# Twelve products of zeros and a written order in the first stage of a two-layer trunk

## The chip, the core and the metric

The kernel runs on one core of one Trainium2 chip. A core has TensorE (PE, matrix products; its weight loads are listed as PEld), VectorE (DVE), ScalarE (ACT), GpSimd (POOL) and SyncE (SP), which here issues nearly all loads. Each engine works through its own list of instructions in order and waits where an operand or a buffer is not ready. The metric is the time of one execution on the device, in microseconds (us).

## The reference

The program takes x (512 tokens of 1024 numbers, f32) through two layers. Each layer is a token mixer and a SwiGLU block; each of these four sub-layers has the same frame:

```python
shift, scale, gate = ada_modulation(c, ada_w, ada_b)   # silu(c) @ w + b, cut in three
h = rms_norm(x, pre_g) * (1.0 + scale) + shift
y = mixer_or_ffn(h)
x = x + gate * rms_norm(y, post_g)
```

The first mixer is an attention: `h @ w_qkv` gives q, k and v (16 heads of 64), a stick-breaking product takes the place of a softmax, and `w_o` projects the result. The second mixer is a gated multiplication over positions. The change touches only what lies ahead of the first attention, and one row of the first gate.

## The kernel before

The tokens lie in four tiles of 128 (`NT`), the features in eight blocks of 128 (`KD`). Products are done in f32 precision by splitting each operand into a high and a low part (`split`: ACT copies the high part, DVE subtracts it from the source for the low part) and adding three products (`mm3`). Weights come in one load each of 512 KB into one of two buffers (`raw`), are split into `wh` and `wl` (`wemit`, DVE at L184), and the next load goes out when a buffer is free. `wget` asks for the next weight.

**The first stage** makes `h`, transposed, and begins q, k and v.

- `norm0(tt)`: ACT squares and sums a tile of x, and takes the root (`sd`); DVE takes the reciprocal (`r`) and scales the tile in place.
- `turn0(tt)`: eight transposes on PE (tile `tp`, L119) into two banks of PSUM, and four copies of 128x256 into `xhT`. For tiles 0 and 1 two copies are ACT's and two DVE's; for tiles 2 and 3 all four are ACT's.
- `row0(raws)`: shift and scale of one block of features, as a row: eight f32 products with one weight column each (tile `ab`; every f32 product shows as two instructions in the trace), a copy of the row by DVE (`row`), and two small products that turn the row into two columns.
- `scales` and `h0`: DVE makes the factors (`ab`) from the columns; ACT writes `hTh` and the scaled `xhT`, DVE subtracts for `hTl`. This is done for block 0 and block 1 from rows; for blocks 2 to 7, `ada0_sum` accumulates on DVE (tile `acc`) and `cols0`/`sums0` reduce on PE.
- `v_step` and `qk0_step` are the products for v (four banks), q and k of the first pair of heads (`pq`, `pk`). All six banks of the tag "b" are then in use.

The order in which an engine takes its instructions is chosen by a planner from estimated durations and readiness, except where the program adds an edge with `order(b, before)`. `Vector`, `Scalar` and `pe_op` have a `chain` flag: while it is set, each new instruction is ordered behind the one before it. In the version before, no chain is set in the first stage; it is set for PE, and later for DVE, from the attention on.

**The gate row.** `Bg` builds a gate, scale or shift row of a later sub-layer in small steps between other work: eight loads of `ada_w` (`rawada`) multiplied into an accumulator on DVE (`ada_stt`), then a load of the row `post_g` or `pre_g` spread over the partitions (tile `g`), and for each half a split (`acch`, `accl`), two products with ones on PE, and DVE's multiplication with `g`. `bg0` builds the first gate, "G0": its eight loads are issued in the first stage, the rest in the attention, where the products go to the banks named `av` and DVE follows a written order.

## Time and profile before

| | us |
|---|---|
| median of 3 runs | 1104.47 (1104.46 to 1104.56) |
| the profiled execution | 1103.49 |
| its span, first to last instruction | 1101.7 |
| PE busy in the span | 1082.1 |
| DVE busy | 972.8 |
| ACT busy | 610.1 |

The three runs lie within 0.1 us of each other; the profiled execution is 1.0 us below their median, and its span 1.8 us below its own time. Rows of the profile begin with start and duration in us when they are in order of time; a bracket at the end tells how long the engine was idle before the row, and what it waited for. `x8` is a count of merged instructions. L89 is the helper by which all of ACT's activations are recorded, L73 that of DVE, L111 that of products, L119 of transposes, L128 of loads.

### The profile page before, as it was taken

To read this page: it belongs to the slowest core of one execution; us is meant where nothing else is said; L and a number is where in the kernel's file an instruction comes from. 1 tells how busy PE (TensorE), PEld (TensorE's weight loads), DVE (VectorE), ACT (ScalarE), POOL (GpSimd) and SP (SyncE) were. 2 spreads that over 40 slices of the span, in tenths; PEclk is the share of its full clock that TensorE was granted. 3 is DMA by queue.
4 is the path that set the end of the run, shared out by engine and by line. 5 is a ranking of instruction groups with operands and counts; after the bars stand their busy time and mean duration, and the time that the engine had idled before them with its cause. 6 is when DMAs were issued, how large, how long until landed. Compare 5 with 4: busy or idle time off the path is not lost.

```text
span 1101.7 us, 18701 instructions
## 1 busy us (share of the span) xinstructions
PE 1082.1 (98%) x7452; PEld 978.7 (89%) x7452; DVE 972.8 (88%) x1293; ACT 610.1 (55%) x1016; POOL 29.5 (3%) x53
## 2 busy tenths in 40 slices
PE   7999999999999999999999999999999999999997
PEld 4787788788999999998888899988999999999996
DVE  4988999866989999989978999868979999899996
ACT  6554665665655555554252767526545555565662
POOL 0020100000000000001000000001000000000000
PEclk9999999999999999999999999999999999999999
DMA  8976434304433434359878324524334342332252
GB/s 317 357 226 218 138 121 131 122 17 153 153 111 124 163 124 153 134 187 347 294 246 322 143 87 137 177 95 163 122 113 153 136 159 100 107 113 96 77 190 78
DMA packets 51355, 176.38 MB, mean 160 GB/s; under 512 B 6074, under 2 KB 9146, under 8 KB 51268
## 3 DMA queue, kind: packets, MB, share of 16 engines
q1 hardware_dynamic: 48708, 166.81, 43.8%
q0 software_dynamic: 2560, 8.39, 2.1%
q8 instruction: 58, 0.95, 0.3%
q14 instruction: 29, 0.24, 0.1%
HBM read 164.69 MB, written 8.39 MB: 157 GB/s over the span
## 4 chain that ended last, share of the span: by engine, by line
PE 85%; DVE 7%; DMA 4%; issue 2%; ACT 2%; SPq 0%; DVEq 0%; ACTq 0%
PE r L111 35%; PE y L111 16%; PE pqk L111 7%; PE X L111 4%; PE gu L111 4%; PE Y L111 3%; PE v L111 3%; PE u L111 2%; PE av L111 2%; PE z L111 2%; PE tw L119 1%; PE Z L111 1%; PE W L111 1%; PE tp L119 1%; DVE wl L184 1%
## 5 line engine op out<-in xcount | busy, mean ns | idle before, releaser
L111 PE MATMUL r<-Sh,wh 128*128 128x256 f32 x640 | 177.3, 277 | 0.6 <-ACT e L89 0.6
L111 PE MATMUL r<-Sl,wh 128*128 128x256 f32 x640 | 177.0, 277 | 0.0
L111 PE MATMUL r<-Sh,wl 128*128 128x256 f32 x640 | 176.9, 277 | 0.0
L89 ACT ACTIVATE wh<-raw 128x1024 fp32r<-128x1024 f32 (+1 forms) x105 | 108.3, 1036 | 101.7 <-DMA raw<-in_wdown 36.1
L111 PE MATMUL y<-wh,as 128*128 128x512 f32 x480 | 150.5, 391 | 0.3 <-DVE svt L73 0.3
L111 PEld LDWEIGHTS r<-Sh,wh 128*128 128x128 f32 x640 | 120.2, 188 | 1.2 <-ACT e L89 1.0
L111 PEld LDWEIGHTS r<-Sl,wh 128*128 128x128 f32 x640 | 120.2, 188 | 0.1
L111 PEld LDWEIGHTS r<-Sh,wl 128*128 128x128 f32 x640 | 120.1, 188 | 0.0
L184 DVE TENSOR_TENSOR wl<-raw,wh 128x1024 fp32r<-128x1024 f32 x79 | 95.9, 1220 | 25.9 <-ACT wh L89 25.7
L73 DVE TENSOR_TENSOR wl<-f,wh 128x1024 fp32r<-128x1024 f32 x95 | 112.9, 1219 | 1.1 <-ACT wh L89 1.1
L89 ACT ACTIVATE wh<-f 128x1024 fp32r<-128x1024 f32 x95 | 100.2, 1055 | 17.3 <-DVE f L73 12.5
L111 PEld LDWEIGHTS y<-wh,as 128*128 128x128 f32 x480 | 90.0, 188 | 19.3 <-issue 0.6
L89 ACT ACTIVATE e<-r 128x256 f32<-128x256 f32 x120 | 45.9, 384 | 102.3 <-PE r L111 100.2
L111 PE MATMUL y<-wl,as 128*128 128x512 f32 x240 | 93.7, 391 | 0.0
L111 PE MATMUL r<-hTh,wh 128*128 128x256 f32 x320 | 88.8, 278 | 0.2 <-DVE gu L73 0.2
L111 PE MATMUL r<-hTh,wl 128*128 128x256 f32 x320 | 88.5, 277 | 0.0
L111 PE MATMUL r<-hTl,wh 128*128 128x256 f32 x320 | 88.5, 277 | 0.0
L111 PEld LDWEIGHTS r<-hTh,wh 128*128 128x128 f32 x320 | 60.1, 188 | 1.1 <-DVE gu L73 0.9
L111 PE MATMUL r<-hTh,b 128*128 128x256 f32 x320 | 60.9, 277 | 0.0
L111 PEld LDWEIGHTS r<-hTl,wh 128*128 128x128 f32 x320 | 60.1, 188 | 0.0
L111 PEld LDWEIGHTS r<-hTh,wl 128*128 128x128 f32 x320 | 60.1, 188 | 0.0
L89 ACT ACTIVATE wh<-rawx 128x1024 fp32r<-128x1024 f32 x40 | 42.5, 1062 | 29.7 <-PE r L111 28.9
(288 smaller groups left out, 2924.3 us busy)
## 6 DMA issues: line engine op xcount, KB each, us to landing
rawada<-in_ada SPq DMA_DIRECT2D x80, 512.0 KB, 6.3
rawy<-in_wy SPq DMA_DIRECT2D x38, 512.0 KB, 4.2
rawx<-in_wx SPq DMA_DIRECT2D x38, 512.0 KB, 3.4
raw<-in_wdown SPq DMA_DIRECT2D x22, 512.0 KB, 5.3
raw<-in_wdn SPq DMA_DIRECT2D x22, 512.0 KB, 3.4
raw<-in_wqk SPq DMA_DIRECT2D x16, 512.0 KB, 4.0
ada<-in_ada0p SPq DMA_DIRECT2D x12, 512.0 KB, 7.6
raw<-in_wgu SPq DMA_DIRECT2D x12, 512.0 KB, 3.5
```

Source lines behind the costliest of these rows:

```text
L73: b = getattr(nc.vector, op)(*args, **kw)
L89: b = nc.scalar.activation(*args, **kw)
L111: b = nc.tensor.matmul(o, l, r, start=start, stop=stop, skip_group_check=True)
L119: last_tp[0] = nc.tensor.transpose(o, i, ident)
L184: last_low[0] = nc.vector.tensor_tensor(l[:], raw[:], h[:].bitcast(F32), ALU.subtract)
```

## The change

Three things are changed.

1. A tile of zeros (128x256) is set by DVE, and `spin(n)` issues n f32 products of it with itself into a bank of their own, which nothing reads. Nine stand ahead of the transposes of tile 0, three between these and the transposes of tile 1.
2. From the first norm on, PE, DVE and ACT follow the order in which the program is written: PE up to the columns of block 0, DVE and ACT up to `h0` of block 0 and the high part of the first q weight. Norms and transposes are cut in two parts so that other work can stand between. The transposes of tiles 2 and 3 stand between the two halves of the first row's products. For all tiles two of the four copies are now DVE's. The low part of the first v weight is ordered behind tile 2's copies and ahead of tile 3's; the low part of the first q weight behind the factors of block 0; the first eight multiply-adds into `acc` behind `hTl` of block 0.
3. For "G0" the load of `g` is issued right behind the last of the eight `rawada` loads, and not when the accumulator is complete.

```diff
+        def row(self, name, s, part):
+
+            if part and name not in self.rows:
+                g = slot(F32, "g", 1, D)[:, 0, :]
+                row = A["pre_g"] if part == 1 else A["post_g"]
+                load(g, row[s : s + 1, :].to_broadcast([P, D]))
+                self.rows[name] = g
+            return self.rows.get(name)
...
                         load(raw, A["ada"][s, part, j % KD])
                         raws.append(raw)
+                        if self.soon and j % KD == KD - 1:
+                            self.row(name, s, part)
...
-                if part:
-                    row = A["pre_g"] if part == 1 else A["post_g"]
-                    g = slot(F32, "g", 1, D)[:, 0, :]
-                    load(g, row[s : s + 1, :].to_broadcast([P, D]))
+                g = self.row(name, s, part)
...
-    bg0, bg = Bg("G0", slots=3, gap=1), Bg("A0", "B0", lag=1, gap=1)
+    bg0, bg = Bg("G0", slots=3, gap=1, soon=True), Bg("A0", "B0", lag=1, gap=1)
...
-                if q and tt < 2:
+                if q:
                     dve.tensor_copy(dst, src)
                 else:
                     act.activation(dst, src, AF.Copy)
...
+    zero = stp.tile([P, 256], F32, name="zero")
+    dve.memset(zero[:], 0.0)
+    zb = bank("zb")
+
+    def spin(n):
+
+        for _ in range(n):
+            mm(zb[:, 0:256], zero[:, 0:P], zero[:], True, True)
...
         for q, raw in enumerate(raws):
+            if q and between is not None:
+                between()
             for k in range(4):
...
-    norm0(0)
-    norm0(1)
-    turn0(0)
-    norm0(2)
-    ab0 = row0(a0)
-    turn0(1)
-    norm0(3)
-    turn0(2)
-    turn0(3)
-    wv0.append(wget(("wv", 0, 0), 0))
+    pe["chain"] = dve.chain = act.chain = True
+    norm0(0)()
+    root = norm0(1)
+    spin(9)
+    turned = turn0(0)
+    root()
+    spin(3)
+    for tt in (2, 3):
+        root = norm0(tt)
+        turned()
+        if tt == 2:
+            turned = turn0(1)
+        root()
+
+    def between():
+        turned = [turn0(tt) for tt in (2, 3)]
+        wv0.append(wget(("wv", 0, 0), 0))
+        for f in turned:
+            f()
+            if f is turned[0]:
+                order(last_low[0], dve.prev)
+                dve.prev = last_low[0]
+
+    ab0 = row0(a0, between)
+    pe["chain"] = False
     a2 = [ada0_raw(2, q) for q in range(4)]
-    h0(scales(ab0, 0), 0, 0)
+    ab = scales(ab0, 0)
+    scaled = dve.prev
+    h0(ab, 0, 0)
+    first = dve.prev
+    wqk0.append(wget(("wqk", 0, 0), 0))
+    order(last_low[0], scaled)
+    dve.chain = act.chain = False
     ab1 = row0(a1)
-    wqk0.append(wget(("wqk", 0, 0), 0))
...
-    acc = ada0_sum(a2, 512, 2)
+    acc = ada0_sum(a2, 512, 2, after=first)
```

`root` and `turned` are the second halves of `norm0` and `turn0`: the root, reciprocal and scaling of a tile, and its copies out of PSUM.

## The prediction

> **What bounds the kernel now.** I read the page first, then what TensorE (PE) waited for, then all engines in order of time up to 31 us, and last the stretch around 90 us.

> ```profile
> span 1101.7 us, 18701 instructions
> PE 1082.1 (98%) x7452; PEld 978.7 (89%) x7452; DVE 972.8 (88%) x1293; ACT 610.1 (55%) x1016; POOL 29.5 (3%) x53
> ...
> PE tp L119 <- DVE x L73: 8.0, 2, 7.3
> PE av L111 <- DVE accl L73: 1.1, 1, 1.1
> ```

> PE is busy for 1082.1 of 1101.7 us. Of its idle time 8.0 us are two waits for the normalised x at the start (7.3 and 0.7), and the next is one of 1.1 us for accl, a half of the gate row. Time is won here only where PE idles or works slowly. The first stage, by PE in order of time, then PE's weight loads around one point:

> ```profile
> 7.31 1.97 PE L119 MATMUL tp<-identt,x 128*128 128x128 f32 x8 [7.31 <-DVE x L73]
> 10.02 1.97 PE L119 MATMUL tp<-identt,x 128*128 128x128 f32 x8 [0.74 <-DVE x L73]
> 11.92 4.96 PE L111 MATMUL ab<-ada,sc 128*1 128x256 f32 x16
> 16.81 0.77 PE L119 MATMUL tp<-identt,x 128*128 128x128 f32 x5
> 17.51 0.60 PE L111 MATMUL ab<-oneb,row 1*128 1x1 f32 x4
> 18.05 1.42 PE L119 MATMUL tp<-identt,x 128*128 128x128 f32 x11
> 19.39 3.61 PE L111 MATMUL ab<-ada,sc 128*1 128x256 f32 x16
> 22.94 0.50 PE L111 MATMUL v<-wh,hTh 128*128 128x512 f32 x1
> ...
> 14.01 0.13 PEld L111 LDWEIGHTS ab<-ada,sc 128*1 128x1 f32 x1 [0.30 <-issue]
> 14.43 0.13 PEld L111 LDWEIGHTS ab<-ada,sc 128*1 128x1 f32 x1 [0.30 <-issue]
> 14.78 0.30 PEld L111 LDWEIGHTS ab<-ada,sc 128*1 128x1 f32 x2 [0.22 <-issue]
> ```

> The same work has two speeds. Each f32 product shows as two passes (eight products, x16). A pass of 256 columns takes 0.42 us up to 14.43 and 0.22 us later (16 from 19.39 to 22.94); a transpose takes 1.90/8 = 0.24 us from 10.02 to 11.92 and 1.34/11 = 0.12 us from 18.05 to 19.39. So PE turns fast at about 14.6 us. The next view, by stretches (columns: us; PE, PEld, DVE, ACT, POOL busy; granted clock; DMA), shows that the granted clock does not tell of it:

> ```profile
> 10.00:14.60 4.60, 4.58 (x15) 2.41 (x16) 3.12 (x8) 4.52 (x11) 0.00 (x0) 1.00 1.03 419
> 19.40:22.90 3.50, 3.50 (x17) 1.25 (x16) 0.69 (x1) 3.44 (x7) 0.00 (x0) 1.00 0.99 405
> 22.00:64.00 42.00, 41.38 (x194) 33.05 (x193) 40.28 (x53) 19.96 (x27) 8.18 (x17) 1.00 0.82 304
> ```

> It reads 1.00 in slow and fast stretches alike; I go by durations. The third row matters most: from 22 to 64 us PE lacks 0.62 us and VectorE (DVE) 1.72 us of 42. An earlier start of v is kept only if DVE starts earlier too. Its rows, with ScalarE's (ACT):

> ```profile
> 13.87 1.06 ACT L89 ACTIVATE wh<-raw 128x1024 fp32r<-128x1024 f32 x1
> 20.23 0.85 ACT L89 ACTIVATE hTh<-xhT,ab 128x512 fp32r<-128x512 f32 x1
> 21.11 0.81 ACT L89 ACTIVATE xhT<-xhT,ab 128x512 f32<-128x512 f32 x1
> ...
> 12.03 0.76 DVE L73 COPY xhT<-tp 128x256 f32<-128x256 f32 x2 [0.30 <-PE tp L119]
> 12.89 0.75 DVE L73 TENSOR_SCALAR x<-x,r 128x1024 f32<-128x1024 f32 x1
> 16.92 0.41 DVE L73 COPY row<-ab 1x256 f32<-1x256 f32 x1 [3.28 <-PE ab L111]
> 17.26 1.20 DVE L184 TENSOR_TENSOR wl<-raw,wh 128x1024 fp32r<-128x1024 f32 x1
> 18.39 0.14 DVE L73 TENSOR_TENSOR ab<-ab,add 128x2 f32<-128x2 f32 x1
> 21.96 0.69 DVE L73 TENSOR_TENSOR hTl<-xhT,hTh 128x512 fp32r<-128x512 f32 x1 [3.23 <-ACT xhT L89]
> 22.90 1.22 DVE L184 TENSOR_TENSOR wl<-raw,wh 128x1024 fp32r<-128x1024 f32 x1 [0.25 <-ACT wh L89]
> 25.62 0.16 DVE L73 TENSOR_TENSOR ab<-ab,add 128x2 f32<-128x2 f32 x1 [0.51 <-PE ab L111]
> ```

> DVE stands idle for 3.28 us and 3.23 us, then runs nearly full from hTl on.

> **The change part by part.**

> *Zero products, start.* One DVE memset of 128x256 is new. No such row exists; around it:

> ```profile
> 0.90 0.07 DVE L73 MEMSET mul<- 128x8 f32 x1
> 5.87 0.17 DVE L73 COPY add<-cols 128x8 f32<-128x8 f32 x1 [4.90 <-DMA cols<-in_cols]
> 32.81 0.52 POOL L788 MEMSET acc<- 128x512 f32 x1 [31.09 <-DVE wl L184]
> ```

> Between 0.07 and 0.52 us; I take 0.4, nearer the larger tile. The mul memset was put ahead of a copy that stands before it in the program and waits for cols, so this memset too should stand near 1 us, in DVE's idle time. PE starts at about 1.4. Nine products are 18 passes, 18 x 0.42 = 7.6 us if all are slow. The open quantity is how long PE must work until it turns fast. From below: 2.7 us (the row passes alone, 11.92 to 14.6). From above: 7.3 us (from the first transpose, 7.31 to 14.6). I take 4.6 (unbroken work from 10.02), since the 0.74 us gap stands ahead of it. Then the turn comes at 6.0, after 10.9 passes, and the other 7.1 x 0.22 = 1.6 end at 7.6. The bounds give a turn at 4.1 with the end at 6.7, and a turn at 8.7 with the end at 8.9. The memory bank of the products is one of six, unused until 10 us; its cost is nothing while the first transposes need four.

> *First transposes.* x of tile 0 is ready at 7.3; eight fast ones take 1.0, so 7.6 to 8.6. The three further products take 6 x 0.22 = 1.3, to 9.9, and hide in the wait for x of tile 1 (10.02, set by its load, unchanged). With the late turn they end at 11.2, which costs 1.2.

> *From 10.02 on, all fast.* Transposes of tile 1: 1.0. Half of the row passes: 8 x 0.22 = 1.75, to 12.8. Sixteen transposes (tiles 2, 3): 1.95, to 14.7; x of tile 3 is there at 13.64. Half of the row passes: 1.75, to 16.5. The four column passes 0.6 and the second row's 16 passes 3.5: v could start at 20.6 for 22.94, **2.4 us earlier**. That holds if the second row's passes fill PE while DVE copies the row, as transposes filled it at 16.81; the written order ends behind the column passes, so they may.

> [...]

> *DVE and ACT.* Four copies of 0.38 move from ACT to DVE. Those of tile 2 lie in the 3.28 us of idle time. Then the written order puts the low half of the first weight (it waits for wh, 14.93, so 14.95 to 16.15) ahead of tile 3's copies (0.76, to 16.9), and the row's copy behind them: at 16.9, no sooner than now. Column passes (0.6) and the two scale steps keep their time (16.92 to 18.39 and two short steps), to 18.75. Then ACT is free (its last copies go at once), so hTh starts at 18.75 instead of 20.23, xhT ends at 20.45, and hTl starts at 20.5 instead of 21.96: **1.5 us**. That is what DVE is given. The eight multiply-adds into acc are now ordered behind hTl; they run behind it today as well, so the order costs nothing. Of the gaps behind hTl (0.25 and 0.51) I count 0.3 as filled by them, since the second weight's low half and the second row no longer all stand ahead. First stage: 1.8 us, between 1.0 (PE held behind the row's copy, below) and 2.4 (PE's own sum). The load of the third weight goes out when its buffer is free, at 16.2 instead of 18.5; DMA is at 0.99 to 1.03 there, so it lands no sooner, and the 4 loads ahead of it in SP's queue had gone by then anyway.

> *The gate row.* Its load moves on SP's queue:

> ```profile
> 42.88 4.25 SPq L128 DMA_DIRECT2D rawada<-in_ada  x5
> 55.62 2.70 SPq L128 DMA_DIRECT2D ones<-in_consts  x6
> ...
> 85.93 0.43 SPq L128 DMA_DIRECT2D g<-in_post_g  x1
> ...
> 90.87 2.28 DVE L73 TENSOR_TENSOR_SCAN left<-ga,ones 128x1025 f32<-128x1025 f32 x1
> 93.97 0.69 DVE L73 TENSOR_TENSOR G<-av,g 128x512 f32<-128x512 f32 x1 [0.82 <-DMA g<-in_post_g]
> 94.58 0.68 DVE L73 TENSOR_TENSOR accl<-G,acch 128x512 fp32r<-128x512 f32 x1
> ...
> 95.31 0.50 PE L111 MATMUL av<-accl,ones 128*128 128x512 f32 x1 [1.10 <-DVE accl L73]
> ```

> It goes out behind the last rawada, at 47.1, where SP next issues at 55.62, and needs its buffer 39 us longer. SP loses nothing, and what stands behind the old place moves up by 0.43. DVE then starts G behind the scan, 0.82 sooner, and accl with it; behind that PE waits 0.3 instead of 1.1. I take **0.8**, between 0 (no buffer free, or another late step) and 1.1.

> *Sum.* 1.8 + 0.8 = 2.6 us. The profiled execution took 1103.49 us (span 1101.7 and 1.8 around it), which becomes 1100.9. The median of the runs, 1104.47, lies 1.0 above it, and becomes **1101.9 us**. About 0.2% (2.2 us) can be told from no change here.

> **The rivals.**

> *Late turn* (1102.7). The products turn PE fast only 7.3 us after their start, and the transposes of tile 1 wait for the last three, to 11.2. The first row then ends at 17.7, its copy waits for PE 0.8 longer than for DVE's own order, and DVE's 1.8 become 1.0: 1.0 + 0.8 = 1.8 won. For it: the first transposes at 7.31 did count for nothing up to 14.6. Against: the gap at 9.28 explains that. [...]

> *PE held in the written order* (1102.7). If the second row's passes go behind the column passes, PE idles from 16.5 to 17.5, 1.0 us; v starts at 21.6, 1.4 early, and the second row, from which DVE makes h of block 1, comes 1.0 later too, so that I count 1.0 won, with G 1.8. For it: those passes stand behind in the program. Against: the present trace fills the same wait with transposes.

> *The gate row wins nothing* (1102.7). Its wait gives way to another (the weights' chain, or a buffer): only 1.8 stays. Against: DVE's 0.82 us name that load alone.

> *Slower: the products stand in the way* (1107.1). Zeros may not turn PE fast. Then nine last to 9.0, eight slow transposes (1.9) to 10.9, three products (2.5) to 13.4, and tile 1 starts 3.4 later than now, with the turn as far behind it as today: 3.4 lost, 0.8 won. It decides from tile 1's start at 12.4 on, where the 2.4 are used up. For it: no product of zeros is in this trace. Against: PE turned fast under passes with one weight column (128*1), so the amount of arithmetic isn't what counts. A late memset would do the same.

> **How the numbers follow.** Forecast 0.50 (own range 1101.2 to 1102.4; 0.42 of it below 1102.26). More than forecast 0.12: both upper bounds, 2.4 + 1.1 = 3.5, or the timed runs, 1.0 us above the profiled one, turned later and win that too (1100.0 to 1101.2). Late turn or PE held 0.16; no gain from the gate row 0.10; slower 0.12. Faster: 0.42 + 0.12 = 0.54. Within 0.2%: 0.08 + 0.16 + 0.10 = 0.34. Slower: 0.12. The range leaves out the slower case: below, 1100.0; above, 1104.2, which holds the small gains and no gain at all.

> **What would show it.** Products from about 1.4 us and their passes dropping from 0.42 to 0.22 before 8 us; tile 1's transposes at 10.0 in 1 us; the first v at 20.6 and hTl at 20.5; the row's copy still near 16.9, with PE busy or idle behind it (that tells the second rival); G's load issued near 45 with no DMA wait, and PE's wait for accl at 0.3. I am wrong if v starts earlier but PE shows new waits for hTl, hTh or weights between 20 and 64 us, or if passes are still slow behind 9 us.

## The result, and the profile after

The changed kernel takes 1107.12 us (median of 9 runs, 1104.54 to 1108.76); the kernel before 1104.47 beside it (9 runs, 1102.29 to 1105.35). The ratio is 1.0029, with a 95% interval of 1.0019 to 1.0038: **slower by 2.7 us**, where 2.6 us less were forecast. The profiled execution took 1108.66 us, 1.5 us above the median; that of the kernel before lies 1.0 us below its own, so the two profiles differ by more than the kernels do. Of all the timed runs below, one counts as slow (1706.28 us, of e15) and stands in no ratio.

The head of the page of the changed kernel:

```profile
span 1106.9 us, 18750 instructions
PE 1088.0 (98%) x7476; PEld 984.2 (89%) x7476; DVE 974.3 (88%) x1298; ACT 609.4 (55%) x1012; POOL 29.6 (3%) x53
```

What its PE waited for (us in total, times, longest):

```profile
PE tp L119 <- DVE t L73: 2.8, 1, 2.8
PE av L111 <- DVE accl L73: 2.4, 1, 2.4
PE tp L119 <- DVE x L73: 1.4, 1, 1.4
```

The span grew by 5.2 us. The wait of 8.0 us for x at the start shrank to 1.4 (and 1.3 for the tile of zeros), but the wait for accl grew from 1.1 to 2.4, and a new one of 2.8 us, for a tile `t`, leads the list. PE in order of time in the first stage of the changed kernel (start, duration):

```profile
1.30 6.26 PE L111 MATMUL zb<-zero 128*128 128x256 f32 x18 [1.30 <-DVE zero L73]
7.41 1.04 PE L119 MATMUL tp<-identt,x 128*128 128x128 f32 x8
8.28 1.46 PE L111 MATMUL zb<-zero 128*128 128x256 f32 x6
11.12 1.09 PE L119 MATMUL tp<-identt,x 128*128 128x128 f32 x8 [1.38 <-DVE x L73]
12.47 1.89 PE L111 MATMUL ab<-ada,sc 128*1 128x256 f32 x8 [0.26 <-DMA ada<-in_ada0s]
14.29 1.97 PE L119 MATMUL tp<-identt,x 128*128 128x128 f32 x16
16.19 1.89 PE L111 MATMUL ab<-ada,sc 128*1 128x256 f32 x8
18.58 0.60 PE L111 MATMUL ab<-oneb,row 1*128 1x1 f32 x4 [0.51 <-DVE row L73]
19.11 3.61 PE L111 MATMUL ab<-ada,sc 128*1 128x256 f32 x16
22.65 0.50 PE L111 MATMUL v<-wh,hTh 128*128 128x512 f32 x1
```

The products do what they are for: all eight transposes of tile 0 take 1.04 us and not 1.97, and everything behind them is fast. Yet v starts at 22.65, only 0.29 us sooner than before. x of tile 1 came 1.1 us later in this execution (11.12 for 10.02), PE waited 0.51 us for the row's copy, and the second row's sixteen passes (19.11) stand behind the column passes.

The second loss is at the gate row. SP's queue, then DVE and PE around the wait for accl:

```profile
41.78 8.22 SPq L128 DMA_DIRECT2D raw<-in_wv  x2
50.05 2.41 SPq L128 DMA_DIRECT2D rawada<-in_ada  x5
52.50 0.44 SPq L128 DMA_DIRECT2D g<-in_post_g  x1
...
92.52 2.29 DVE L73 TENSOR_TENSOR_SCAN left<-ga,ones 128x1025 f32<-128x1025 f32 x1
94.72 0.67 DVE L73 TENSOR_TENSOR G<-av,g 128x512 f32<-128x512 f32 x1
95.31 0.68 DVE L73 TENSOR_TENSOR accl<-G,acch 128x512 fp32r<-128x512 f32 x1
...
96.05 0.50 PE L111 MATMUL av<-accl,ones 128*128 128x512 f32 x1 [2.43 <-DVE accl L73]
```

DVE no longer waits for g, so that part works. But the whole scan comes 1.65 us later (92.52 for 90.87). The planner has put one more weight load (`raw<-in_wv` is now x2) ahead of the five rawada loads, and this load waits for its buffer: the five go out at 50.05 instead of 42.88, and the multiply-adds for the gate, and all that DVE does behind them, follow. PE is 0.74 us later than before (96.05 for 95.31).

The third loss is far from the change. DVE and PE around 600 us in the changed kernel, then the same in the kernel before:

```profile
593.76 1.29 DVE L73 SCALAR_TENSOR_TENSOR B<-rawada,sc,B 128x1024 f32<-128x1024 f32 x1 [0.77 <-DMA rawada<-in_ada]
...
601.46 1.28 DVE L73 SCALAR_TENSOR_TENSOR B<-rawada,sc,B 128x1024 f32<-128x1024 f32 x1 [2.96 <-DMA rawada<-in_ada]
...
612.61 1.25 PE L119 MATMUL tp<-identt,t 128*128 128x128 f32 x7 [2.78 <-DVE t L73]
```

```profile
591.50 1.28 DVE L73 SCALAR_TENSOR_TENSOR B<-rawada,sc,B 128x1024 f32<-128x1024 f32 x1
...
598.11 1.28 DVE L73 SCALAR_TENSOR_TENSOR B<-rawada,sc,B 128x1024 f32<-128x1024 f32 x1 [1.95 <-DMA rawada<-in_ada]
...
608.89 1.09 PE L119 MATMUL tp<-identt,t 128*128 128x128 f32 x8 [0.26 <-DVE t L73]
```

Here DVE builds a row of a later sub-layer (B2) between the splits of the weights. Each multiply-add waits for its own load, and what stands behind it on DVE, the tile `t` among it, waits too. In the changed kernel two of them wait, 0.77 and 2.96 us, against one of 1.95; PE stands for 2.78 us instead of 0.26 and is now 3.72 us behind.

The last 1.7 us come from the clock. The granted clock by stretches of 3.41 us (columns: us; PE, PEld, DVE, ACT, POOL busy; granted clock; DMA share; GB/s):

```profile
606.36:609.77 3.41, 3.41 (x16) 2.54 (x14) 2.95 (x4) 1.45 (x5) 0.55 (x1) 1.00 1.01 378
609.77:613.19 3.42, 0.64 (x6) 0.58 (x6) 2.20 (x6) 2.39 (x7) 0.00 (x0) 1.00 0.68 277
613.19:616.60 3.41, 3.41 (x12) 2.83 (x11) 3.25 (x7) 2.42 (x5) 0.14 (x1) 0.50 0.00 0
616.60:620.01 3.41, 3.41 (x17) 2.78 (x16) 3.22 (x6) 2.15 (x7) 0.40 (x1) 1.00 0.39 156
```

In the stretch in which PE waited it was busy for 0.64 of 3.42 us; in the next one the granted clock is 0.50, and PE's products of 128x512 start 0.43 us apart, against 0.23 from 616.98 on. So PE's rows, matched one by one with those of the kernel before, are 0.7 us late at 96 us, 3.7 at 612 and 5.3 at 617; the span is 5.2 longer.

### The profile page after: what moved, and what is told of

Same layout as the page of the kernel before. It is cut to its first block, busy times and chain, and to the rows that moved or that the text cites. A ratio compares the mean times of both kernels' runs of the same rounds, so it can differ in the third digit from the quotient of the medians.

```text
span 1106.9 us, 18750 instructions
## 1 busy us (share of the span) xinstructions
PE 1088.0 (98%) x7476; PEld 984.2 (89%) x7476; DVE 974.3 (88%) x1298; ACT 609.4 (55%) x1012; POOL 29.6 (3%) x53
## 4 chain that ended last, share of the span: by engine, by line
PE 84%; DVE 6%; DMA 6%; issue 2%; ACT 2%; SPq 1%; DVEq 0%; ACTq 0%
PE r L111 35%; PE y L111 15%; PE pqk L111 7%; PE X L111 4%; PE Y L111 3%; PE v L111 3%; PE gu L111 3%; PE u L111 2%; PE av L111 2%; PE z L111 2%; PE tw L119 1%; PE Z L111 1%; PE W L111 1%; DMA rawada<-in_ada 1%; DVE wl L184 1%
## 5 line engine op out<-in xcount | busy, mean ns | idle before, releaser
L111 PE MATMUL r<-Sh,wh 128*128 128x256 f32 x640 | 177.1, 277 | 0.6 <-ACT e L89 0.6
L111 PE MATMUL r<-Sl,wh 128*128 128x256 f32 x640 | 176.7, 276 | 0.0
L111 PE MATMUL r<-Sh,wl 128*128 128x256 f32 x640 | 176.6, 276 | 0.0
L89 ACT ACTIVATE wh<-raw 128x1024 fp32r<-128x1024 f32 (+1 forms) x105 | 108.3, 1037 | 100.0 <-DMA raw<-in_wdown 31.2
L111 PE MATMUL y<-wh,as 128*128 128x512 f32 x480 | 151.5, 393 | 0.3 <-DVE svt L73 0.2
L111 PEld LDWEIGHTS r<-Sh,wh 128*128 128x128 f32 x640 | 120.1, 188 | 1.2 <-ACT e L89 1.0
L184 DVE TENSOR_TENSOR wl<-raw,wh 128x1024 fp32r<-128x1024 f32 x79 | 96.0, 1221 | 27.9 <-ACT wh L89 27.7
L111 PEld LDWEIGHTS r<-Sl,wh 128*128 128x128 f32 x640 | 120.2, 188 | 0.1
L111 PEld LDWEIGHTS r<-Sh,wl 128*128 128x128 f32 x640 | 120.1, 188 | 0.0
L73 DVE TENSOR_TENSOR wl<-f,wh 128x1024 fp32r<-128x1024 f32 x95 | 113.0, 1221 | 1.3 <-ACT wh L89 1.3
L89 ACT ACTIVATE wh<-f 128x1024 fp32r<-128x1024 f32 x95 | 100.3, 1055 | 17.8 <-DVE f L73 12.7
L111 PEld LDWEIGHTS y<-wh,as 128*128 128x128 f32 x480 | 90.7, 189 | 19.7 <-issue 0.6
L89 ACT ACTIVATE e<-r 128x256 f32<-128x256 f32 x120 | 46.0, 385 | 102.7 <-PE r L111 100.7
L111 PE MATMUL y<-wl,as 128*128 128x512 f32 x240 | 94.1, 392 | 0.0
L111 PE MATMUL r<-hTh,wh 128*128 128x256 f32 x320 | 88.7, 277 | 0.2 <-DVE gu L73 0.2
L111 PE MATMUL r<-hTl,wh 128*128 128x256 f32 x320 | 88.4, 276 | 0.0
L111 PE MATMUL r<-hTh,wl 128*128 128x256 f32 x320 | 88.4, 276 | 0.0
L111 PEld LDWEIGHTS r<-hTh,wh 128*128 128x128 f32 x320 | 60.1, 188 | 1.1 <-DVE gu L73 0.9
L111 PE MATMUL r<-hTh,b 128*128 128x256 f32 x320 | 61.0, 276 | 0.0
L111 PEld LDWEIGHTS r<-hTl,wh 128*128 128x128 f32 x320 | 60.1, 188 | 0.0
L111 PEld LDWEIGHTS r<-hTh,wl 128*128 128x128 f32 x320 | 60.1, 188 | 0.0
L89 ACT ACTIVATE wh<-rawx 128x1024 fp32r<-128x1024 f32 x40 | 42.5, 1062 | 29.7 <-PE r L111 29.0
```

Source lines behind the costliest of these rows:

```text
L73: b = getattr(nc.vector, op)(*args, **kw)
L89: b = nc.scalar.activation(*args, **kw)
L111: b = nc.tensor.matmul(o, l, r, start=start, stop=stop, skip_group_check=True)
L184: last_low[0] = nc.vector.tensor_tensor(l[:], raw[:], h[:].bitcast(F32), ALU.subtract)
```

## The experiments

The kernel before stood beside every run; its medians were 1104.52, 1104.02, 1104.07 and 1104.44 in the four sessions with timed runs. Three theories are named in what was expected. Queue theory: a weight load that now stands ahead of the gate row's loads on SP's queue costs the time. Late-chain theory: what the first stage wins is lost at later places where PE waits for DVE, ACT or a load. The third: the products cost time by themselves.

### The parts of the change alone

**e1** is the changed kernel without the products and without the sooner load of g: only the written order is left.

```diff
-    bg0, bg = Bg("G0", slots=3, gap=1, soon=True), Bg("A0", "B0", lag=1, gap=1)
+    bg0, bg = Bg("G0", slots=3, gap=1), Bg("A0", "B0", lag=1, gap=1)
...
-    spin(9)
...
-    spin(3)
```

> The change without the twelve products and without the sooner load of g: the written order alone. Queue theory: the order by itself moves a weight load ahead of the five loads for the gate row in SP's queue, so the gate row is late, PE waits about 2 us or more for accl near 95 us, and the median is 2 to 4 us above before (ratio 1.002 to 1.004). Late-chain theory: the stage up to 100 us costs under 1 us, and what is above that is a wait of PE for t near 610 us. Theory that the products cost the time: without them the ratio is at or below 1.000.

**e2** is the kernel before with the twelve products, PE's order fixed only around them:

```diff
+    pe["chain"] = True
+    spin(9)
     turn0(0)
+    spin(3)
+    pe["chain"] = False
```

> Before with the twelve products alone, in a written order on PE only as far as the first transposes. SP's queue is as before. Queue theory: passes are fast from 8 us on, v starts 1 to 2 us sooner, PE's wait for accl stays near 1.1, ratio 0.998 to 0.9995. Theory that the products cost the time: tile 1's transposes start later than before and the ratio is 1.001 to 1.003. Late-chain theory: as the queue theory up to 100 us, and anything else shows near 610 us.

**e3** is the kernel before with g's load moved (`soon`, as in the change) and nothing else.

> Before with the sooner load of g alone. All three theories: SP's queue differs by this load only, DVE does not wait for it, PE's wait for accl falls from 1.1 to 0.3, 0.8 us won, ratio 0.999 to 1.000. If the load in the full stretch near 47 us hurts, the ratio is above 1.000 and a wait of DVE for rawada near 55 us shows it.

**e4** is the whole change with one edge more: that weight load stays behind the last of the rawada loads, as before.

```diff
+        b = load(raw[:], src)
+        if len(raws) == 7:
+            order(b, last_ada[0])
```

> The changed kernel with one edge more: the weight load that moved ahead is ordered behind the last of the eight loads for the gate row, as before the change. Queue theory: the loss is gone, PE's wait for accl is 0.3 to 0.6, v starts 0.3 to 1.5 us sooner than before, ratio 0.998 to 0.9995. Late-chain theory: the first 100 us gain 1 us against the changed kernel (1.0029), and the ratio stays above 1.001 because of the wait near 610 us. Theory that the products cost the time: ratio near 1.003 as with the change.

Measured: e1 1107.16 (ratio 1.0026, 1.0013 to 1.0040), e2 1105.92 (1.0016, 1.0003 to 1.0030), e3 1104.11 (1.0000, 0.9990 to 1.0010), e4 1105.42 (1.0007, 0.9997 to 1.0017). No part makes the kernel faster. The edge takes 1.7 us off the changed kernel's 1107.12, which is from another session with the same time of the kernel before, and the two intervals do not overlap. The wait for accl is 1.0 in e4, against 2.4. With the edge alone the change is no longer told apart from the kernel before, but it is not faster either: e4 lies between what the queue theory (at most 0.9995) and the late-chain theory (over 1.001) expected.

The time of e1 is the one that the queue theory expected, but its wait for accl is 1.29 us, not 2 or more. Its profiled execution, 1104.55, is 2.6 us below its median, so it does not show where the time goes. e2's ratio lies in the range of the theory that the products cost time by themselves (1.001 to 1.003).

e2 is the surprise: in its profile the products alone gain more in the first stage than the whole change, and the time is longer. In order of time, PE's start of v and DVE at 296 us in e2:

```profile
21.31 0.50 PE L111 MATMUL v<-wh,hTh 128*128 128x512 f32 x1
...
295.98 1.23 DVE L73 TENSOR_TENSOR f<-rawx,rawy 128x1024 f32<-128x1024 f32 x1 [2.47 <-DMA rawx<-in_wx]
```

The same row in the kernel before:

```profile
296.28 1.22 DVE L73 TENSOR_TENSOR f<-rawx,rawy 128x1024 f32<-128x1024 f32 x1 [0.73 <-DMA rawx<-in_wx]
```

The longest of PE's waits in e2, and two of its stretches behind that (columns as above):

```profile
PE r L111 <- ACT e L89: 2.4, 1, 2.4
```

```profile
313.94:317.35 3.41, 1.06 (x9) 0.86 (x8) 3.21 (x7) 1.09 (x4) 0.00 (x0) 1.00 0.14 58
317.35:320.76 3.41, 3.41 (x18) 3.41 (x17) 0.11 (x1) 0.39 (x1) 0.00 (x0) 0.50 0.00 0
```

v starts at 21.31, 1.63 us sooner than in the first profile of the kernel before. Instruction by instruction PE stays 1.6 us ahead up to the wait for accl, which is 0.5 us shorter, and 2.1 us ahead from there to 314 us. There DVE has been nearly full since 296 us, when it had waited 2.47 us for a load (0.73 in the kernel before); so ACT's `e` comes only 0.3 us sooner, PE waits 2.35 us, and the stretch behind runs at half the clock. Before the wait PE was 2.1 us ahead, behind the slow stretch it is 1.3 behind.

### First relief of the late waits

If the late waits take the gain back, it should come through where they are gone. **e5** is the kernel before with two reliefs: sums of the first two block pairs on GpSimd, and every third rawada tile of B2 in a slot of its own. **e6** adds the products, **e7** is e4 with the reliefs, **e8** the whole change with them.

```diff
-                        if self.slots:
+                        if self.slots or ((name, at) == ("B", 2) and j % KD % 3 == 2):
...
+        add = nc.gpsimd if len(got) - first_blocks[0] in (0, 1) else dve
-        dve.tensor_tensor(f24[:, 0:4, :], f13[:, 0:4, :], xr[:, 4:8, :], ALU.add)
+        add.tensor_tensor(f24[:, 0:4, :], f13[:, 0:4, :], xr[:, 4:8, :], ALU.add)
```

> The kernel before with two late stretches relieved and nothing else: the four 128x512 sums of the first two block pairs (f24, at 297 to 310 us) go from VectorE to GpSimd, and every third row-weight tile of B2 (567 to 600 us) gets a slot of its own in place of one of two shared buffers. Nothing of the change is in it. All theories expect PE's gaps at 317 us (0.59 before) and 609 us (0.26 before) under 0.5 each, and, since the two gaps are small in the kernel before, a time of 1103.0 to 1104.5. It is the base for the three kernels beside it; only if the sums are slow on GpSimd (over 2.5 us each) would it be later than before.

> The kernel of the run before in this list, and the twelve products of zeros around the first transposes; the instructions behind the first 25 us are in the same order in both. Late-chain theory (the 2.1 us that the products win are taken back at 317 and 609 us, where PE waits for a chain on VectorE set by landings, and a granted clock under 1 behind the wait takes more): with both stretches relieved the gain goes through, so 1.5 to 2.2 us under the kernel beside it, about 1101.5. Theory that the products cost time by themselves, wherever it is lost: 1 to 2 us over the kernel beside it, as without the relief (1105.92 against 1104.52). If the chains were only partly relieved: within 1 us of it.

> The whole change with the weight load put back behind the five row-weight loads, and both late stretches relieved. Late-chain theory: the first stage's gain (0.7 to 1.7 us on PE up to 300 us in the run without the relief) goes through, 0.7 to 1.7 under the kernel that has the relief alone. The rival, that the written order costs time for another reason behind 320 us: as late against that kernel as the run without relief was against before (+0.9).

> The whole change as it is, with both late stretches relieved. Queue theory beside the late-chain theory: PE's wait for accl at 94 us is 2.4 instead of about 1.0 with the weight load ahead of the five row-weight loads, so 1.0 to 1.7 us over the run with that load put back, and within 1 us of the kernel with the relief alone. If the order on the queue costs nothing: equal to the run with the load put back.

Measured: e5 1108.50 (ratio 1.0037, 1.0026 to 1.0048), e6 1106.15 (1.0013, 1.0005 to 1.0022), e7 1107.44 (1.0028, 1.0019 to 1.0038), e8 1108.92 (1.0040, 1.0027 to 1.0052). The base missed: it is 4.5 us slower than before. Two rows of e5 tell why, a sum on GpSimd and ACT in the chain at 604 us:

```profile
308.85 4.01 POOL L294 TENSOR_TENSOR f<-f,rawx 128x512 f32<-128x512 f32 x1 [9.61 <-DVE wl L73]
...
604.12 0.63 ACT L89 ACTIVATE b<-rawy 128x512 fp32r<-128x512 f32 x1 [2.69 <-DMA rawy<-in_wuy]
```

This sum takes 4.01 us (the same sum of the first pair 1.29), so PE still waits 0.94 us at 316; and with rawada out of the way the next weights' loads moved up, ACT waits for one of them ahead of the same chain, and PE waits 2.59 us at 608. The reliefs moved the waits. This profile is e5's fastest run, 2.8 us below its median, so it need not show all of the loss. The differences against this base are as the theories expected, though: the products are worth 2.35 us (e6 to e5), e7 is 1.06 us under e5, and the weight load put ahead of the gate row costs 1.48 (e8 to e7, whose intervals overlap). With e4 that makes two pairs for the order on the queue, 1.7 and 1.5 us.

### Second relief

**e9**: the kernel before, with the sums of the first pair alone on GpSimd and the last two of B2's eight loads and multiply-adds left out. **e10** is that with the products, **e11** the whole change with it.

```diff
+                def cut(j):
+                    return group[j // KD][:2] == ("B", 2) and j % KD > 5
...
-                    if i >= 0:
+                    if i >= 0 and not cut(i):
```

> The kernel before with a smaller relief, since the one of the earlier base put a wait for the rows of the next weights ahead of the same chain: the last two of the eight row-weight loads and multiply-adds of B2 are left out (the kernel leaves that part of the computation out), and the two sums of the first block pair alone go to GpSimd. Nothing of the change is in it. All theories: the multiply-adds that wait for their rows at 598 us are gone, so PE's gap at 609 us is under 0.5; the gap at 317 us under 0.6; time 1102.5 to 1104.5. It is the base for the two kernels beside it.

> The kernel of the run before in this list (the same two loads and multiply-adds left out) and the twelve products of zeros; the order behind 25 us is the same. Late-chain theory: the products' 2.1 us reach the end, 1.5 to 2.2 us under that kernel, and PE's gaps at 317 and 609 us stay under 1 us each. Theory that the products cost time by themselves: 1 to 2 us over it. If only the chain at 609 us was relieved and that at 317 us was not: 0 to 1 us under it, with a gap of over 1.5 us at 317 us.

> The whole change as it is, with the same relief (the same two loads and multiply-adds left out). Queue theory and late-chain theory together: the first stage wins 0.3 to 1.7 us on PE, the wait for accl takes back 1.3, and nothing is lost at 317 and 609 us: within 1 us of the kernel with the relief alone, instead of 2.7 us over the kernel before as without it. The rival (the written order costs in another place): 2 to 3 us over it.

**e12** keeps all work: the products, the sooner load of g, and B2's last step moved to the next sub-layer.

```diff
-            if bg2 is not None and k >= mid - 3 and k != mid - 1:
+            if bg2 is not None and k >= mid - 3 and k != mid - 1 and k < nk - J - 1:
```

> A whole kernel: the twelve products of zeros, the gate row's load sooner, the order on the queue as before, and one step of B2's row weights (its last load and multiply-add) moved from the products with the down weights to the next sub-layer, so that no multiply-add waits on VectorE at 598 us. Late-chain theory: 2.1 us won in the first stage, 0.4 to 0.8 at 94 us, some of it lost at 317 us, nothing at 609 us: 1102.0 to 1103.5. Theory that the products cost time by themselves: 1105 to 1106.5. If the moved step takes its wait along to the next sub-layer: about 1104.5.

Measured: e9 1103.60 (0.9997, 0.9987 to 1.0007), e10 1104.22 (1.0003, 0.9991 to 1.0014), e11 1106.99 (1.0026, 1.0016 to 1.0036), e12 1106.02 (1.0021, 1.0011 to 1.0032). The base is as expected; its gaps at 317 and 609 us are gone. e10, e11 and e12 miss the late-chain theory. e11 lies 3.4 us over e9, nearest to its rival (the written order costs in another place, 2 to 3 us), and e12 in the range of the theory that the products cost time by themselves; e10 (0.6 us over e9) is in no range. In e10 too the two gaps are gone, but the next place of this kind takes over, at 711 us, where DVE and ACT feed short products. Its granted clock there:

```profile
711.05:714.47 3.42, 1.89 (x11) 1.19 (x9) 3.42 (x7) 2.46 (x3) 0.00 (x0) 1.00 0.44 153
714.47:717.88 3.41, 3.17 (x8) 2.48 (x8) 3.41 (x9) 0.63 (x1) 0.00 (x0) 0.50 0.93 346
```

Two waits, 0.91 and 0.63 us, lie in one stretch, and the clock falls. So relieving single places was no clean test. What costs e11 its 3.4 us its profile does not show: it is e11's fastest run, 2.8 us below the median, and without such a fall. By the mean granted clocks of the timed runs, 3.8 us are lost at half clock in e11 and 1.7 in e9, so some 2 us of it are the clock.

### Filling the wait, and a base that leaves nothing out

**e13** and **e14** put twelve useless transposes on PE at about 600 us, in the changed kernel and in the kernel before:

```diff
+            if s == 1 and q == 0 and 2 not in filled:
+                filled.append(2)
+                for _ in range(12):
+                    chained = pe["prev"]
+                    transpose(ps[:, 0:P], ident)
+                    order(last_tp[0], chained)
```

> The whole change, and twelve more transposes (of the identity, into the bank that the next real transposes write) on PE behind the first tile's products at 600 us: about 1.45 us of useless work at 0.12 each, ahead of the place where PE waited 2.78 us at 609. Late-chain theory: the wait there is set by VectorE, so the filling comes out of the wait (2.8 to about 1.3) and costs nothing: within 0.7 of the change's 1107.1; and if the waits' second price is the granted clock that falls behind them (0.82 to 0.84 over 610 to 620), a shorter wait trips it less often: up to 1.7 us under it. Theory that PE sets the time there: 1.45 us over it, 1108.5.

> The kernel before with the same twelve transposes at 600 us. PE waits only 0.26 us there, so the filling lies on PE's path: 1.0 to 1.4 us over before, about 1105.7, under every theory in which PE sets the time of before there. If the late chain alone set the time in the kernel before too: equal to before, 1104.2 to 1104.7.

**e15** is the kernel before with `soon`, the first pair's sums on GpSimd and B2's last step moved (edits shown above); **e16** adds the products.

> The kernel before with the gate row's load sooner, the two sums of the first block pair on GpSimd, and one step of B2's row weights moved to the next sub-layer; without the products of zeros; nothing is left out. The base for the kernel beside it. Late-chain theory: the gaps at 317 and 609 us stay under 0.5 and what is left waits at 711 us: 1103.0 to 1104.5.

> The kernel of the run before in this list and the twelve products of zeros; the order behind 25 us is the same. Late-chain theory with three such places (317, 609 and 711 us): two are relieved, the third is not, so 0 to 1.5 us of the products' 2.1 us reach the end, 1102.0 to 1104.0, and where the granted clock falls it falls around 711 us. Theory that the products cost time by themselves: 1 to 2 us over the kernel beside it.

Measured: e13 1109.99 (7 runs, 1105.85 to 1114.60; ratio 1.0050, 1.0029 to 1.0072), e14 1105.68 (1.0012, 1.0000 to 1.0023), e15 1106.53 (1.0011, 1.0000 to 1.0022), e16 1104.29 (0.9994, 0.9985 to 1.0004). e14 costs 1.24 us, as it should where PE sets the time. e13 was to be free and was not: against the changed kernel's 1107.12 it costs 2.9 us, in another session and with a wide spread. Its gap at 609 us is gone, as expected; but the filling stands ahead of tile 1's products, on which DVE waits as well, so it is no clean delay of PE alone. The products are worth 2.24 us on top of e15 by the medians, 1.15 by the means of the runs that stand in the ratios. But e15, as e5, missed as a base: it was to take 1103.0 to 1104.5 and is slower than the kernel before, and its profile, which is its fastest run (1102.22), does not show why. e16 ends just above its range, and its one fall of the clock before the end of the kernel comes at 715 us, as expected. No whole kernel is faster than the one before beyond its interval; e16 and e3 equal it.

One pair of these kernels is a clean relief of one place. e12 and e16 have the same products, the same load of g and the same moved step, and differ only in the sums of the first pair on GpSimd. PE's wait at 317 us is 1.47 us in e12 and under 0.12 in e16, and the ratio falls from 1.0021 to 0.9994, with intervals that do not overlap. Against the kernel before of its own session e12 is 1.95 us slower and e16 0.15 faster: 2.1 us, where the wait alone would make 1.4. Neither profile has a fall of the clock right behind it.

### A second look at each kernel

**e17** and **e18** are the changed kernel and the kernel before, unaltered, one execution each: 1110.11 and 1104.87 us. The first is longer than all nine timed runs of the changed kernel.

> The changed kernel unaltered, for a second look at one execution. If the long landings and the gap of 2.78 us at 609 us belong to the kernel: a gap of 2 us or more there again, and rows for B2 that take over 6 us. If they belong to the execution: a gap of 0.3 to 2 us, as in the other kernels with the same late order (1.49, 1.80). In both cases the wait for accl at 94 us is 2.0 to 2.7 again, since the order on the queue sets it, and the granted clock changes at times that differ by whole multiples of 3.41 us, from an offset of its own; it falls to one half behind a wait only where over about 1.6 us of one such stretch of 3.41 us is idle.

> The kernel before unaltered, for a second look at one execution. If its small gaps (0.59 at 317 us, 0.26 at 609 us) belong to the kernel: under 0.8 at both again. If to the execution: up to 2.4 at 609 us (the one with the filling had 0.92 behind 1.45 of filling). PE turns to its full rate between 9.5 and 16 us, wherever its 3.41 us stretches happen to end; no fall of the granted clock before 1090 us unless a gap is over 1.6 us.

What PE waited for in e17, then in e18:

```profile
PE av L111 <- DVE accl L73: 2.7, 1, 2.7
PE tp L119 <- DVE t L73: 2.0, 1, 2.0
PE r L111 <- ACT e L89: 1.7, 2, 1.4
```

```profile
PE r L111 <- ACT e L89: 0.7, 1, 0.7
PE av L111 <- DVE accl L73: 0.7, 1, 0.7
PE tp L119 <- DVE t L73: 0.5, 1, 0.5
```

The waits repeat: at 94 us 2.43 and 2.66 us in the changed kernel against 1.10 and 0.65; at 609 us 2.78 and 2.00 against 0.26 and 0.53. They belong to the kernel more than to the execution. What the same wait for accl costs differs, by where it lies in the stretches. In e17 (first two rows) and in the first profile of the changed kernel (last three):

```profile
91.75:95.16 3.41, 1.11 (x5) 0.56 (x3) 3.41 (x4) 2.11 (x4) 0.00 (x0) 1.00 0.55 161
95.16:98.57 3.41, 3.05 (x7) 2.47 (x8) 3.41 (x5) 0.00 (x0) 0.00 (x0) 0.50 0.27 59
```

```profile
90.95:94.36 3.41, 2.67 (x12) 1.88 (x10) 2.98 (x2) 3.32 (x6) 0.00 (x0) 1.00 0.39 127
94.36:97.77 3.41, 1.72 (x7) 1.42 (x8) 3.41 (x6) 0.11 (x1) 0.00 (x0) 1.00 0.28 109
97.77:101.18 3.41, 3.41 (x16) 2.82 (x15) 3.03 (x3) 0.70 (x1) 0.00 (x0) 1.00 0.62 173
```

In e17 2.30 us of the wait fall into one stretch, and the next runs at 0.50. In the other execution the border cuts the wait into 0.74 and 1.69, and the clock stays at 1.00. e17 against e18 gives the account of one pair of executions, PE's rows matched one by one: 2.1 us ahead when v starts (21.91 for 23.97) and 2.5 at 51; the wait for accl takes 2.0 and the clock behind it some 1.5, which makes +1.1; 0.3 is lost before 300 us; 317 us takes 0.9; at 609 us the wait takes 1.5 and the clock 1.5. The spans differ by 5.2 us (1108.3 and 1103.1).

## Why the prediction was wrong

**Right.** The tile of zeros was set at 0.98 in 0.27 us, PE started at 1.30. Products of zeros do turn PE fast: the eighteen passes took 6.26 us, to 7.56 (forecast 7.6), the first transposes lasted to 8.45, the further three products to 9.74 (9.9). That 7.56 meets 7.6 so closely is in part luck: in the twelve profiles with the products the eighteen passes end at 6.99 to 8.16 us. Transposes take 0.13 to 0.14 us (1.09 and 1.04 for eight) once PE is fast, against 1.97 for eight from 10.02 in the kernel before. DVE no longer waits for g.

**"First stage: 1.8 us".** This term was too large, because the kernel before was read from one execution. There PE turned fast at 14.7 us. In the seven profiles that have the first stage of the kernel before without products, the turn comes at 10.9 to 16.3 us, and the later it comes, the later v starts: at 20.93 (turn at 10.87, e15), 21.47 (12.12, e5), 22.15 (13.08, e9), 22.94 (14.69), 23.43 (14.94, e3), 23.77 (15.73, e14) and 23.97 (16.30, e18), in the mean 22.67. With the products alone v starts at 21.23 to 22.36 (five profiles, mean 21.74), with the written order as well at 21.71 to 22.65 (seven, mean 22.02). So v gains 0.9 us by the products and 0.65 by the change; hTl, on which the term rested, comes 1.0 sooner (20.73 for 21.69), not 1.5. One pair of profiles can show anything from a gain of 2.7 us (e2 to e18) to a loss of 0.8 (e16 to e15).

**"x of tile 1 (10.02, set by its load, unchanged)."** It differs by a microsecond between executions: PE waited for it until 10.02, 10.31 and 10.50 in the kernel before, e1 and e18, until 11.12 in the changed kernel, and in e2, e4 and e17 took it at 9.92 to 10.29 almost without a wait (0.15 in e4). The first profile of the changed kernel had a late one; its hTl starts at 21.36, and its row's copy at 18.11, not 16.9.

**The written order.** "The second row's passes fill PE while DVE copies the row" failed: they stand behind the column passes, PE waits 0.51 us, and DVE gets the second row later. This was the second rival, and its wait is there, 0.5 us of the 1.0 that it priced. The written order brought nothing beyond the products: v starts at 21.74 in the mean with the products alone and at 22.02 with the order too; in e1, with the order alone, at 23.05.

**"SP loses nothing."** Failed, and for a reason that no line of the diff names. SP's queue in the stage behind is not written down but planned; the planner reacted to the new order by putting a weight load, which waits 8 us for its buffer, ahead of the five loads of the gate row. I costed the load that was moved in the text and not the ones that the planner would move. Price: 1.7 us (the change with and without e4's edge) and 1.5 (e8 and e7). The same order on the queue is in e1 and not in e2 or e3, so it comes from the written order, not from the products or from g. It makes 1.7 of the 2.7 us by which the changed kernel is slower.

**The gate row.** "DVE's G 0.82 sooner" held in e3 alone: PE's wait for accl fell from 1.10 (0.65 in e18) to 0.18. The time did not change (1.0000, 0.9990 to 1.0010).

**The step that turned the sign** is the last one of the sum, "1.8 + 0.8 = 2.6 us", taken off the end as if PE set the time all the way. Being busy for 98% of the span, PE seemed to. But PE has ten waits of 0.17 to 1.1 us in the kernel before. Beside the one for accl, the four that lie between 220 and 610 us are:

```profile
PE av L111 <- DVE ar L73: 0.8, 1, 0.8
PE r L111 <- ACT e L89: 0.6, 1, 0.6
PE av L111 <- ACT ar L89: 0.4, 1, 0.4
...
PE tp L119 <- DVE t L73: 0.3, 1, 0.3
```

They mark places where DVE, ACT and the loads are as late as PE is. An earlier PE waits there, and not between 20 and 64 us, where the prediction looked for new waits (0.31 and 0.22 us in the changed kernel, 0.31 and 0.23 before). The wait for `e` at 317 us is 0.6 here and 2.35 in e2, that for `t` at 609 us 0.3 here and 1.1 in e2. And where PE was idle for 1.78 us or more of one 3.41 us stretch, ten times in the 20 profiles, the next stretch ran at 0.50 each time, which by the length of a stretch costs some 1.7 us more. The timed runs bear out the part of the clock without any profile, since each has its mean granted clock, given to 0.001 or 1.1 us. Of 131 runs of the kernel before, 9 have a mean of 0.997 or less; of the changed kernel 7 of 9, of e2 6 of 11, of e1 4 of 9, of e4 2 of 11, of e3 none of 11. Span times one minus that mean is an estimate of the time lost at half clock, the end of the kernel included: 1.8 us in the mean for the kernel before, 2.0 for e4, 3.4 for the changed kernel and for e2. So of the 2.7 us between the means (1107.05 and 1104.33) the clock makes about 1.7, and waits, less what the first stage wins, the other 1.1. This is another cut through the same 2.7 us than the price of the queue, whose wait for accl is one of those that make the clock fall. For e2 the clock makes about all of its 1.6, so its waits eat up about what the first stage wins. For e4 it makes 0.2 of 1.1.

**The rivals.** The slower one was priced at 1107.1, which is the time measured, but its mechanism, zeros that do not turn PE, is not what happened; that the number fits is luck. "The gate row wins nothing" was right in effect. No rival held a late wait and the clock behind it, although the list of PE's waits, of which the prediction shows the first two rows, has those waits.

**Open.** Why the loads are later at 296 and at 590 us in the kernels with the products. Between 575 and 600 us the loads moved 312 to 319 GB/s in the five profiles without products that have the same work there (both of the kernel before, e1, e3, e14) and 292 to 304 in the five with them (both of the changed kernel, e2, e4, e13); the order on SP's queue is the same there. Part of this is the place of the window: moved along with PE's rows, which are up to 3.7 us later in the second group, it gives 311 to 319, and 295 to 302 with e13 at 318. And what the products change in the time depends on what stands behind them: +1.4 us in the kernel before, -2.35 in e6, +0.6 in e10, -2.24 in e16 (-1.15 by the means), with the same 0.9 us won in the first stage in the mean. The two that gain do so on bases that are themselves slower than the kernel before, by 4.5 and 2.1 us. That these differences are the waits and the clock is shown for single executions; that they are nothing else is not. And why the written order costs 2.8 us on top of e10 (e11) and 1.2 on top of e2 (the change), of which the queue makes some 1.6, stays open.

## What to carry to other kernels

Read the start of a kernel from several executions before pricing a gain there: here v started at 20.93 to 23.97 us, the later the later PE had turned fast (10.87 to 16.30). A gain early in a kernel is worth what the last shared wait lets through: before adding it up, list every later place where the busiest engine already waits a little, and ask who is late there. Price such a wait with the clock behind it: here a stretch of 3.41 us with 1.78 us or more of PE idle was followed by one at 0.50 ten times of ten, one with 0.95 to 1.68 us once in 22. When a part of a program's order is left to a planner, compare the queues of the whole program after an edit, not only the lines edited.

## What the runs showed of the hardware

**Loads.** The same 512 KB load is not the same in two executions: the second rawx at 296 us landed 4.3 us after its issue in the kernel before and 6.1 in e2, behind the same orders on SP's queue, counted to the start of DVE's sum that waits for it.
